# Output weights of two gated networks: the rest of the split written by ScalarE and an accumulating transfer, and 15 instead of 12 block tiles

## The chip, the cores and the metric

The kernel runs on one core of a Trainium2 chip. The metric is the device time of one execution in microseconds (us), the median over several executions. Engines are named as the profile names them: PE is TensorE (matrix products; PEld is its weight load), DVE is VectorE, ACT is ScalarE, POOL is GpSimd, SP is SyncE, which in this kernel issues almost all transfers.

## The reference

Two decoder layers run over 512 tokens of width 1024, in float32. Layer 0 mixes tokens with a state-space model, layer 1 with forgetting attention, and each is followed by a gated network ("ConvFFN"). The change touches only the two gated networks:

```python
def conv_ffn(h, w_up, conv_w, conv_b, w_down):
    up = h @ w_up                       # 1024 -> 2 x 2816
    a, b = jnp.split(up, 2, axis=-1)
    S = a.shape[1]
    ap = jnp.pad(a, ((0, 0), (CONV_W - 1, 0), (0, 0)))
    a_conv = conv_b
    for i in range(CONV_W):             # causal, width 3
        a_conv = a_conv + ap[:, i:i + S] * conv_w[i]
    return (jax.nn.silu(a_conv) * b) @ w_down      # 2816 -> 1024
```

Before each network a modulation (shift, scale and gate, three 1024 x 3072 products of a conditioning vector) and an RMS norm are applied; after it, the result times the gate is added to the residual.

## The kernel before, in words

**Products in two parts.** Every float32 product is made of three faster ones. A weight tile is split into a rounded part `hi` (type float32r) and a rest `lo = w - hi`; activations likewise. `mms` (L300) issues three matmuls for each 128-row slice: `hi` with the activation's `hi`, `hi` with its `lo`, and `lo` with its `hi`. `put_parts` (L285) does the split: ACT writes `hi` (L287, an Activate with Copy), then DVE writes `lo = src - hi` (L288, a Tensor Tensor). `split` (L272) takes the two buffers, has SP load the raw weights (`raw`, L187), and calls `put_parts`; `weights` (L290) does this for one output tile of 128 columns.

**Buffers.** Raw weights go through 3 buffers (`raw`), `hi` and `lo` through 5 each (`w_hi`, and `w_lo0` to `w_lo4` in turn). A tile's buffer is free again when PE has finished the tile that stood five places earlier in the order.

**The gated network** (`ffn`, L597). The 2816 hidden channels are 22 tiles of 128, numbered f = 0 to 21. For each f the two up products (a and b) are made in one of two ways:

- *Whole*: `product` (L308) with `self.weights` for 2 outputs of 8 slices. On PE 2 x 8 x 3 products, each in two halves of 256 tokens, which are 96 matmuls of 256 columns. On ACT two `hi` of 1024 elements, on DVE two `lo`.
- *Block* (`quarters`, L529): a Strassen-like scheme in which seven products of quarter blocks take the place of eight: 7 x 4 x 3 = 84 matmuls of 256 columns. Sums and differences of weight blocks are made by DVE (four `sums`, L537), four operands are split (`w_hi<-raw`, two `w_hi<-sums`, and one quarter `a22`), ACT copies four products out of PSUM (`nm_h`, L573) and DVE adds them (`nm_t`, L537). PE goes on accumulating into a product's PSUM bank after ACT has copied it.

`WHOLE_TILES` lists the whole tiles of each network. Before the change it is f = 0 to 4, 8, 11, 14, 17, 20 in the first network (12 block tiles) and 0 to 3 in the second (18 block tiles).

The hidden tiles are gathered in groups of 6, 5, 6 and 5 (`GROUPS`). While the up products of group q are made, the down products of group q - 1 are made between them: 8 output tiles (`down`, matmuls of 512 columns, 18 of them for a group of six and 15 for a group of five), one or two after each f. So 24 of a network's 32 down weight tiles come between up tiles, and the last group's 8 come at the end. DVE then also adds the result to the residual (L378). In the first network, DVE further computes two rows of a later modulation (`ada_units`, L256) after each f from 6 on.

**Order.** The tile framework decides the order of instructions on each engine when the program is built; instructions of later tiles stand between those of earlier ones. Each engine then runs its list in order, waiting on semaphores. GpSimd's list has nothing in the gated networks but small memsets that fix addresses.

Of the kernel before, what the change touches and what calls it, by code (L numbers as in the profile page):

```python
# [8 lines left out]
F32 = mybir.dt.float32  # L9
F32R = mybir.dt.float32r  # L10
I32 = mybir.dt.int32
AF = mybir.ActivationFunctionType
ALU = mybir.AluOpType
# [32 lines left out]
ROWS_FROM = 0  # L46
GROUPS = (6, 5, 6, 5)
TAIL = 4
WHOLE_TILES = (0, 1, 2, 3, 4, 8, 11, 14, 17, 20), (0, 1, 2, 3)
SUMS = (0,) * 6 + (2,) * 16  # L50
FIRST = (("c", (KT,)), ("s5_prm", (3, G // 2)))
REST = (
# [11 lines left out]
class Trunk:  # L64
# [6 lines left out]
    def __init__(self, tc, io, ctx):  # L71
        self.tc, self.nc, self.io, self.ctx = tc, tc.nc, io, ctx
        nc = self.nc
        pool = lambda name, bufs, **k: ctx.enter_context(tc.tile_pool(name=name, bufs=bufs, **k))
        self.const = pool("const", 1)
        self.act = pool("act", 1)
        self.wpool = pool("wpool", 3)
        self.tmp = pool("tmp", 2)
        self.small = pool("small", 2)
        self.dram = pool("dram", 1, space=DRAM)  # L80
        self.mm = pool("mm", 4, space=PSUM)
        self.aux = pool("aux", 4, space=PSUM)
        self.bg, self.late = [], ()
        self.acc = None
        self.pending = None
        self.rests, self.odd = 0, False

        self.ones = self.const.tile([P, P], F32, name="ones")
        nc.vector.memset(self.ones, 1.0)
        self.sc = self.const.tile([P, KT], F32, name="sc")  # L90
        self.ada = pool("ada", 1)
        self.crow = self.ada.tile([P, D], F32, name="ada_c")
        self.sc32 = self.const.tile([P, KT, 32], F32, name="sc32")

        self.sel = self.const.tile([P, 6], F32, name="sel")
        nc.gpsimd.memset(self.sel, 0.0)
        for q in range(4):
            for c in (q, 4 + q % 2):
                nc.gpsimd.memset(self.sel[32 * q:32 * q + 1, c:c + 1], 1.0)
        self.par = [self.const.tile([P, 24], F32, name=f"par{i}") for i in range(4)]  # L100
        self.ga = [self.const.tile([P, KT], F32, name=f"ga{i}") for i in range(4)]
# [170 lines left out]
    def split(self, src, shape, pool=None, bufs=WB, off=None):  # L272

        if off:
            more = TAIL_ROOM - math.prod(shape[1:])
            hi, lo = (self.wide(pool, n, {"bufs": bufs}, F32R, more, off[n], shape) for n in ("w_hi", "w_lo"))
        elif pool:
            hi, lo = (pool.tile(shape, F32R, name=n, bufs=bufs) for n in ("w_hi", "w_lo"))
        else:
            hi = self.wpool.tile(shape, F32R, name="w_hi", bufs=WB)  # L280
            lo = self.rest(shape, odd=self.odd)
        self.put_parts(hi, lo, self.raw(shape, src))
        return hi, lo

    def put_parts(self, hi, lo, src):  # L285
# [311 lines left out]
    def ffn(self, i, l, x, nxt, whole, sums=()):  # L597

        nc, tc = self.nc, self.tc
        with tc.tile_pool(name=f"ffn{l}", bufs=1, reuse_waits="tile") as pool:  # L600
            first = [sum(GROUPS[:q]) for q in range(len(GROUPS) + 1)]
            keep, g = {}, {}

            def gate_room(q):
                g[q] = [pool.tile([P, GROUPS[q], S], F32R, name=n, tag=f"{n}{q % 2}") for n in ("ghi", "glo")]

            self.gap(pool, 32, "g_gap")
            gate_room(0)
            b = [pool.tile([P, KT // 2, S], F32, name=f"x{j}", tag=n) for j, n in enumerate(("ghi1", "glo1"))]
            conv = pool.tile([P, 4, FT], F32, name="conv_wb")  # L610
            nc.sync.dma_start(conv, self.io["conv"][l])
            cw, cb = conv[:, :3], conv[:, 3]

            def gated(m, ps, cols):
                f = m // 2
                if m % 2 == 0:
                    t = pool.tile([P, S], F32, name="conv", bufs=2)
                    nc.scalar.activation(t, ps, AF.Identity, bias=cb[:, f:f + 1], scale=cw[:, 2, f:f + 1])
                    for d in (1, 2):
                        nc.vector.scalar_tensor_tensor(  # L620
                            t[:, d:], ps[:, :S - d], cw[:, 2 - d, f:f + 1], t[:, d:], op0=ALU.mult, op1=ALU.add
                        )
                    nc.scalar.activation(t, t, AF.Silu)
                    keep[f] = t
                    return
                t = keep.pop(f)
                nc.vector.tensor_tensor(t, t, ps, ALU.mult)
                q = sum(f >= n for n in first[1:])
                j = f - first[q]
                if q not in g:  # L630
                    gate_room(q)
                hi, lo = g[q]
                self.put_parts(hi[:, j, :], lo[:, j, :], t)

            after, y = nxt

            def up(fs, **k):
                self.odd = True
                self.product(
                    self.io["w_up"][l], range(2 * fs[0], 2 * fs[-1] + 2), KT, x, gated, apart=True, **k  # L640
                )
                self.odd = False

            last = len(GROUPS) - 1
            down = lambda q, ms, **k: self.product(
                self.io["w_down"][l][:, :, first[q]:first[q + 1], :], ms, GROUPS[q], g[q],
                self.add_residual(i, q == last), after=after, **k
            )
            todo, ready = [], {}
            for q, n in enumerate(GROUPS):  # L650
                for j, f in enumerate(range(first[q], first[q + 1])):
                    if f == 0:
                        up([0, 1], head=3)
                        todo.append(self.forms_x(pool, x, b))
                    elif f in whole:
                        if f > 1:
                            up([f], ready=ready)
                            ready = {}
                        if todo and f + 1 in whole:
                            self.odd = True  # L660
                            ready = {m: self.weights(self.io["w_up"][l][m], KT) for m in (2 * f + 2, 2 * f + 3)}
                            self.odd = False
                        for _ in range(3):
                            if todo and next(todo[0], True):
                                todo.pop()
                    else:
                        while todo:
                            if next(todo[0], True):
                                todo.pop()
                        self.quarters(pool, l, f, x, gated)  # L670
                    if q:
                        down(q - 1, range(j * KT // n, (j + 1) * KT // n))
                    self.tick(sums[f] if f < len(sums) else 0)
            self.done()
            down(last, range(KT), tail=TAIL, tail_pool=(pool, 4, TAIL_OFF))
        return y
# [827 lines left out]
def build(tc, io, out, stop=None):  # L1504
    with ExitStack() as ctx:
# [5 lines left out]
        k.bg = [k.ada_units(2, [0, 1]), k.ada_units(2, [2]), k.ada_units(3, [2])]  # L1511
        x = k.ffn(1, 0, x, k.norm_mod(2), WHOLE_TILES[0], SUMS)
        if stop == "ffn0":
# [3 lines left out]
        if stop == "fox":  # L1517
            return k.dump(out)
        k.ffn(3, 1, x, k.norm_out(out), WHOLE_TILES[1])
        k.finish_norm()  # L1520
# [82 lines left out]
```

## Time and profile before

| | |
|---|---|
| runs | 1197.50, 1193.79, 1190.88 us; median 1193.79 |
| the profiled execution | 1197.65 us; its span from first to last instruction 1195.9 us |
| granted TensorE clock, mean | 0.991 |
| PE busy | 1174.1 us (98%) |
| DVE busy | 988.7 us (83%) |
| ACT busy | 592.4 us (50%) |
| POOL busy | 62.6 us (5%) |
| DMA traffic | 183.83 MB, 154 GB/s mean |

The first network's up products begin at about 254 us and its last down product ends at about 602 us; the second's run from about 846 to 1186 us. A matmul's row in the profile is longer than the distance to the next row, because matmuls are pipelined: a 256-column matmul shows 276 ns but the next begins about 114 ns later. So PE's time is read from the distance between starts, or from windows, and not from the sum of its rows. In a table of windows each engine has its busy time in the window, with the number of its instructions in brackets, then the granted clock as a share, the DMA engines' busy share and what they moved. In a table of lines the number after the bar is the busy time in us, then the mean duration of one in ns, then the idle time ahead of them and what ended it.

### The profile page before, as it was taken

What the parts mean: (1) busy time and instruction counts of PE and PEld (TensorE: products, weight loads), DVE (VectorE), ACT (ScalarE), POOL (GpSimd) and SP (SyncE); (2) the same over time, 40 slices, a digit from 0 to 9 for tenths busy, and PEclk for the clock granted to TensorE, in tenths of its full rate; (3) what the DMA queues carried; (4) which work ended last, traced back from release to release, by engine and by line L of the source; (5) the groups of instructions that cost most, each with busy time, mean ns of one, the idle gap of its engine ahead of it and who ended that gap; (6) DMA issues with size and microseconds to landing.
All of it is one profiled execution on the core that took longest, in us unless ns stands there. A gap on an engine that the chain in (4) does not pass through costs nothing.

```text
span 1195.9 us, 21116 instructions
## 1 busy us (share of the span) xinstructions
PE 1174.1 (98%) x8243; PEld 1026.5 (86%) x8243; DVE 988.7 (83%) x1824; ACT 592.4 (50%) x1069; POOL 62.6 (5%) x114
## 2 busy tenths in 40 slices
PE   7999999999999999999999999999999999999997
PEld 2455687899999999999899788878999999999987
DVE  8899977889888888887776788866899888888855
ACT  2554525346544454453453566554466555555543
POOL 1000000000000000000000443330000000000000
PEclk9999989999999999999999999999999999999999
DMA  9687758822264455554514655523123342343331
GB/s 359 226 256 251 230 167 303 295 92 89 87 204 131 159 174 170 185 184 139 194 36 138 209 185 166 200 76 97 47 75 96 124 124 86 111 124 95 104 88 72
DMA packets 73234, 183.83 MB, mean 154 GB/s; under 512 B 23231, under 2 KB 25503, under 8 KB 72111
## 3 DMA queue, kind: packets, MB, share of 16 engines
q1 hardware_dynamic: 72847, 181.96, 46.6%
q8 instruction: 65, 1.06, 0.4%
q10 hardware_dynamic: 288, 0.52, 0.1%
q14 instruction: 34, 0.28, 0.1%
HBM read 175.53 MB, written 6.92 MB: 153 GB/s over the span
## 4 chain that ended last, share of the span: by engine, by line
PE 86%; DVE 7%; DMA 3%; ACT 2%; issue 1%; POOL 0%; SPq 0%; DVEq 0%; ACTq 0%; POOLq 0%
PE mmp L304 42%; PE mmp L566 15%; PE aux L566 6%; PE mmp L1167 4%; PE mmp L1344 3%; PE mmp L1197 2%; DVE w_lo L288 2%; PE aux L1490 2%; PE aux L1473 1%; PE aux L1061 1%; PE aux L1053 1%; PE mmp L221 1%; PE aux L1443 1%; ACT w_hi L287 1%; DMA raw<-in_w_down 1%
## 5 line engine op out<-in xcount | busy, mean ns | idle before, releaser
L287 ACT ACTIVATE w_hi<-raw 128x1024 fp32r<-128x1024 f32 (+4 forms) x197 | 176.0, 900 | 146.9 <-PE mmp L304 75.5
L288 DVE TENSOR_TENSOR w_lo<-raw,w_hi 128x1024 fp32r<-128x1024 f32 (+4 forms) x197 | 203.4, 1036 | 29.7 <-ACT w_hi L287 25.2
L304 PE MATMUL mmp<-a_hi,w_hi 128*128 128x256 f32 (+1 forms) x600 | 185.9, 311 | 0.0
L304 PE MATMUL mmp<-a_hi,w_lo 128*128 128x256 f32 (+1 forms) x600 | 182.8, 306 | 0.0
L304 PE MATMUL mmp<-a_lo,w_hi 128*128 128x256 f32 (+1 forms) x600 | 182.7, 305 | 0.0
L304 PE MATMUL mmp<-ghi,w_hi 128*128 128x512 f32 (+1 forms) x392 | 143.9, 367 | 0.0
L304 PE MATMUL mmp<-glo,w_hi 128*128 128x512 f32 (+1 forms) x392 | 143.9, 367 | 0.0
L304 PE MATMUL mmp<-ghi,w_lo 128*128 128x512 f32 (+1 forms) x392 | 143.6, 366 | 0.0
L304 PEld LDWEIGHTS mmp<-a_hi,w_hi 128*128 128x128 f32 x600 | 112.4, 188 | 7.6 <-issue 2.6
L304 PEld LDWEIGHTS mmp<-a_hi,w_lo 128*128 128x128 f32 x600 | 112.5, 188 | 6.4
L304 PEld LDWEIGHTS mmp<-a_lo,w_hi 128*128 128x128 f32 x600 | 112.6, 188 | 4.8
L287 ACT ACTIVATE w_hi<-sums 128x1024 fp32r<-128x1024 f32 x68 | 71.6, 1060 | 65.9 <-DVE sums L537 27.4
L566 PE MATMUL mmp<-w_hi 128*128 128x256 f32 x360 | 99.6, 277 | 0.0
L566 PE MATMUL mmp<-w_hi,w_lo 128*128 128x256 f32 x360 | 99.5, 276 | 0.0
L566 PE MATMUL mmp<-w_lo,w_hi 128*128 128x256 f32 x360 | 99.4, 276 | 0.0
L288 DVE TENSOR_TENSOR w_lo<-sums,w_hi 128x1024 fp32r<-128x1024 f32 x68 | 82.4, 1220 | 7.6 <-ACT w_hi L287 6.5
L256 DVE CUSTOM_DVE_ANT_0 ada_raw<-ada_raw,ada_c,rest 128x1024 f32<-128x1024 f32 x64 | 83.7, 1326 | 5.1 <-DMA ada_raw<-in_ada_rows 5.1
L304 PEld LDWEIGHTS mmp<-ghi,w_lo 128*128 128x128 f32 x392 | 73.6, 188 | 12.3
L304 PEld LDWEIGHTS mmp<-ghi,w_hi 128*128 128x128 f32 x392 | 73.6, 188 | 11.2
L304 PEld LDWEIGHTS mmp<-glo,w_hi 128*128 128x128 f32 x392 | 73.6, 188 | 11.1
L378 DVE SCALAR_TENSOR_TENSOR h<-mmp,par,h 128x512 f32<-128x512 f32 (+1 forms) x98 | 62.9, 649 | 23.4 <-PE mmp L304 23.3
L566 PEld LDWEIGHTS mmp<-w_hi 128*128 128x128 f32 x360 | 67.6, 188 | 0.1
(317 smaller groups left out, 2833.0 us busy)
## 6 DMA issues: line engine op xcount, KB each, us to landing
raw<-in_w_up SPq DMA_DIRECT2D x88, 512.0 KB, 3.4
ada_raw<-in_ada_rows SPq DMA_DIRECT2D x64, 512.0 KB, 4.2
raw<-in_ada_w SPq DMA_DIRECT2D x32, 512.0 KB, 5.5
raw<-in_w_down SPq DMA_DIRECT2D x32, 384.0 KB, 3.2
raw<-in_w_down SPq DMA_DIRECT2D x32, 320.0 KB, 3.1
nf<-nfd SPq DMA_DIRECT2D x8, 1152.0 KB, 5.7
raw<-in_fox_qk SPq DMA_DIRECT2D x16, 512.0 KB, 3.2
h<-in_x SPq DMA_DIRECT2D x8, 512.0 KB, 5.5
```

The source lines that it names most:

```text
L221: self.last_mm = nc.tensor.matmul(ps[32 * qq:32 * qq + 32, :], self.sc32[:, k, :], w[:, q * S:(q + 1) * S], start=(step is steps[0]), stop ...
L256: nc.vector.tensor_tensor_reduce(w, w, self.crow, 1.0, self.ada_b[:, i, m:m + 1], ALU.mult, ALU.add, self.par[i][:, m:m + 1])
L287: nc.scalar.activation(hi, src, AF.Copy)
L288: self.late = (nc.vector.tensor_tensor(lo, src, hi.bitcast(F32), ALU.subtract).ins,)
L304: self.last_mm = self.nc.tensor.matmul(o, wt, xt[:, cols], start=(k == 0 and n == 0), stop=(k == nk - 1 and n == 2),)
L378: self.nc.vector.scalar_tensor_tensor(h, v, self.par[i][:, 16 + m:17 + m], h, op0=ALU.mult, op1=ALU.add,).ins,
L566: self.last_mm = nc.tensor.matmul(o, wt[:, k], xt[:, k], start=(first and k == 0 and n == 0), stop=(k == H - 1 and n == 2), skip_group_che ...
L1053: nc.tensor.matmul(yp[g2][:, k, :], t[:, 2 * k + g2], u[:, g, :], start=(k == 0), stop=False, skip_group_check=True,)
L1167: nc.tensor.matmul(ps, w[m][:, k, :], x[:, k], start=(k == 0), stop=(k == KT - 1))
L1197: nc.tensor.matmul(gps[m], wt, xt[:, k], start=(k == 0 and part == 0 and xt is yhi), stop=(k == KT - 1 and part == 1))
L1344: self.last_mm = nc.tensor.matmul(ps[q, b][:, :n], xt[:, k, tb], wt, start=(k == 0 and i == 0), stop=(k == KT - 1 and i == 2),)
L1490: nc.tensor.matmul(pv[:, c * P:], self.v[:, hp, k, r].rearrange("p t d -> p (t d)"), pp[:, r, c + 3 * k:NB + 3 * k, :].rearrange("p b t -> ...
```

## The change

Two things are changed. For the 24 down tiles of each network that are made between up tiles (48 in all), `lo` is no longer made by DVE: ACT writes `-hi` into `lo`'s buffer with a second Activate, and then a transfer issued by GpSimd reads the weights from DRAM once more and adds them to what stands there, which gives `w - hi`. The last group's down tiles, and all up tiles, are split as before. And the first network's whole tiles are now 0 to 4, 10 and 16, so that tiles 8, 11, 14, 17 and 20 become block tiles and 10 and 16 whole ones: 15 block tiles for 12.

```diff
-WHOLE_TILES = (0, 1, 2, 3, 4, 8, 11, 14, 17, 20), (0, 1, 2, 3)
+WHOLE_TILES = (0, 1, 2, 3, 4, 10, 16), (0, 1, 2, 3)
...
-        self.rests, self.odd = 0, False
+        self.rests, self.odd, self.by_dma = 0, False, False
...
             hi = self.wpool.tile(shape, F32R, name="w_hi", bufs=WB)
             lo = self.rest(shape, odd=self.odd)
-        self.put_parts(hi, lo, self.raw(shape, src))
+        t = self.raw(shape, src)
+        if self.by_dma:
+            self.nc.scalar.activation(hi, t, AF.Copy)
+            self.nc.scalar.activation(lo, hi.bitcast(F32), AF.Copy, scale=-1.0)
+            self.nc.gpsimd.dma_start(lo, src, accum_op=ALU.add)
+        else:
+            self.put_parts(hi, lo, t)
         return hi, lo
...
                     if q:
+                        self.by_dma = True
                         down(q - 1, range(j * KT // n, (j + 1) * KT // n))
+                        self.by_dma = False
```

On PE the order of the work stays, but for the five tiles that become block tiles and the two that become whole ones. On ACT and POOL the lists move as follows. ACT, first network, at the tiles of the second group (`conv`, `ghi` and `nm_h` belong to the up tiles, `w_hi<-raw 128x640` are the down weights), before:

```order
L573 ACTIVATE nm_h<-aux 128x256
L287 ACTIVATE w_hi<-raw 128x512
L287 ACTIVATE w_hi<-raw 128x640
L623 ACTIVATE conv<-conv 128x512
L287 ACTIVATE ghi<-conv 128x512
L287 ACTIVATE w_hi<-raw 128x640
L573 ACTIVATE nm_h<-mmp 128x256 x2
```

and with the change (line numbers are higher by six behind the new lines; L284 is `hi`, L285 is `-hi`):

```order
L579 ACTIVATE nm_h<-aux 128x256
L293 ACTIVATE w_hi<-raw 128x512
L284 ACTIVATE w_hi<-raw 128x640
L285 ACTIVATE w_lo<-w_hi 128x640
L629 ACTIVATE conv<-conv 128x512
L284 ACTIVATE w_hi<-raw 128x640
L293 ACTIVATE ghi<-conv 128x512
L285 ACTIVATE w_lo<-w_hi 128x640
L579 ACTIVATE nm_h<-mmp 128x256 x2
```

Each down tile now has a second instruction on ACT, right behind `hi` or with one instruction of an up tile between them; the copies `nm_h` of the next block tile stand behind it.

POOL, the first network, before:

```order
L136 MEMSET x_gap 128x16
L136 MEMSET ehi_gap 128x16
L136 MEMSET v_gap 128x32
```

and with the change:

```order
L136 MEMSET x_gap 128x16
L136 MEMSET ehi_gap 128x16
L286 DMA w_lo<-in_w_down 128x768 x8
L286 DMA w_lo<-in_w_down 128x640 x8
L286 DMA w_lo<-in_w_down 128x768 x8
L136 MEMSET v_gap 128x32
```

The 24 transfers stand in POOL's list with nothing between them, in the order in which PE uses the tiles; in the second network they stand the same way, at the end of the list.

## The prediction

> **What bounds the kernel now.** I read the page's busy shares first, then the chain of waits over a piece of the first network, then windows over both networks.
>
> ```profile
> PE 1174.1 (98%) x8243; PEld 1026.5 (86%) x8243; DVE 988.7 (83%) x1824; ACT 592.4 (50%) x1069; POOL 62.6 (5%) x114
> ```
>
> ```profile
> 25 pieces in order of time: start us, us, what
> 459.81 2.75 PE mmp L566 x24
> 462.56 1.36 PE aux L566 x12
> 463.92 2.72 PE mmp L566 x24
> 466.64 1.36 PE aux L566 x12
> 468.00 1.36 PE mmp L566 x12
> 469.36 3.42 PE mmp L304 x15
> ```
>
> ```profile
> 310.30:564.00 253.70, 253.70 (x1863) 238.99 (x1862) 216.20 (x320) 119.38 (x178) 0.52 (x1) 1.00 0.51 165
> 891.00:1148.00 257.00, 256.71 (x1882) 241.67 (x1882) 221.93 (x329) 140.40 (x221) 0.00 (x0) 1.00 0.35 109
> ```
>
> The chain names nothing but PE in the gated networks: one product follows the other, at a granted clock of 1.00. In the window of the first network PE is busy for 253.70 of 253.70 us, in that of the second for 256.71 of 257.00. DVE is busy for 85% and 86% of them, ACT for 47% and 55%, the DMA engines for 0.51 and 0.35, POOL has nothing. So the time of both networks is the number of matmuls times their distance, and work taken from DVE is by itself worth nothing: what can be won is what PE is spared.
>
> **The change part by part.** *Three more block tiles.* A whole tile (96 matmuls), the down tile after it, a block tile (84 matmuls) and its down tile, in windows of the first network:
>
> ```profile
> 445.32:456.23 10.91, 10.91 (x97) 10.91 (x96) 8.93 (x14) 3.42 (x4) 0.00 (x0) 1.00 0.59 185
> 456.23:459.65 3.42, 3.42 (x18) 2.82 (x16) 2.54 (x5) 0.76 (x2) 0.00 (x0) 1.00 0.07 29
> 459.65:469.20 9.55, 9.55 (x86) 9.55 (x84) 9.09 (x13) 5.16 (x8) 0.00 (x0) 1.00 0.55 175
> 469.20:472.61 3.41, 3.41 (x17) 2.82 (x16) 2.95 (x6) 2.44 (x5) 0.00 (x0) 1.00 0.04 15
> ```
>
> 10.91 - 9.55 = 1.36 us a tile, 12 matmuls at 0.114 us. Three tiles: **4.1 us** less. It is the only term on the path.
>
> *DVE.* Its groups in the first network from the second group's up tiles on (329.4 to 564 us):
>
> ```profile
> L288 DVE TENSOR_TENSOR w_lo<-raw,w_hi 128x1024 fp32r<-128x1024 f32 x19 | 23.1, 1222 | 1.6 <-ACT w_hi L287 1.2
> L288 DVE TENSOR_TENSOR w_lo<-sums,w_hi 128x1024 fp32r<-128x1024 f32 x19 | 23.1, 1221 | 4.3 <-ACT w_hi L287 4.2
> L288 DVE TENSOR_TENSOR w_lo<-raw,w_hi 128x768 fp32r<-128x768 f32 x15 | 14.3, 954 | 0.6 <-ACT w_hi L287 0.5
> L537 DVE TENSOR_TENSOR sums<-raw 128x512 f32<-128x512 f32 x18 | 11.9, 688 | 4.1 <-DMA raw<-in_w_up 4.1
> L537 DVE TENSOR_TENSOR nm_t<-mmp,nm_h 128x256 f32<-128x256 f32 x30 | 11.8, 418 | 0.0
> L288 DVE TENSOR_TENSOR w_lo<-raw,w_hi 128x640 fp32r<-128x640 f32 x10 | 8.2, 821 | 0.7 <-ACT w_hi L287 0.7
> L288 DVE TENSOR_TENSOR w_lo<-raw,w_hi 128x512 fp32r<-128x512 f32 x10 | 6.9, 686 | 0.0
> ```
>
> Removed: 16 rests of 954 ns and 8 of 821 ns, 21.8 us a network. Added: a block tile has one rest from raw (1.22), two from sums (2.44), a quarter's (0.69), four sums (4 x 0.69) and four additions (4 x 0.42), 8.8 us, a whole tile two rests (2.44): 6.3 us more, 19.0 for three. The first network's DVE load falls by 2.8 us, the second's by 21.8. On the path both are 0, since PE covers them. Blocks now come five in a row (5 to 9, 11 to 15, 17 to 21) where they came in pairs, but each leaves DVE 1.2 us less to do, so a run should build up no more lag than a pair did. The 0.3 us for which PE is not busy in the second network may go; I leave it at 0.
>
> *ACT.* The window of ACT's work about a block tile and PE's need of it:
>
> ```profile
> 466.17 0.36 ACT L573 ACTIVATE nm_h<-mmp 128x256 f32<-128x256 f32 x1
> 473.60 0.72 ACT L287 ACTIVATE w_hi<-raw 128x640 fp32r<-128x640 f32 x1
> 474.23 0.37 ACT L573 ACTIVATE nm_h<-mmp 128x256 f32<-128x256 f32 x1
> 483.88 0.85 ACT L287 ACTIVATE w_hi<-raw 128x768 fp32r<-128x768 f32 x1 [1.60 <-DMA raw<-in_w_down]
> ```
>
> ```profile
> 467.84 0.28 PE L566 MATMUL mmp<-w_hi 128*128 128x256 f32 x1
> 486.03 0.39 PE L304 MATMUL mmp<-ghi,w_lo 128*128 128x512 f32 x1
> ```
>
> `-hi` has the shape of `hi`: 16 x 0.85 + 8 x 0.72 = 19.4 us more a network. A block tile's four operands and four copies are another 3.2 us more than a whole tile's two operands (the windows above: 5.16 against 3.42 in PE's time alone, the rest beside the down tiles), some 10 us for three. ACT goes from 119.4 to about 149 us in the first network, below 60%, and in the second from 140.4 to 160, 62%. That is no bound, but ACT runs in order: `-hi` stands in front of the copies `nm_h` of the next block tile, and PE waits for these before it goes on in their bank. The copy of 466.17 ends at 466.53 and PE needs it at 467.84: 1.3 us to spare. One `-hi` of 0.72 to 0.85 fits into that. Cost 0; if two come together, 0.4 us at such a tile.
>
> *The transfer.* Its `lo` must be there when PE reads it. The tile whose `hi` starts at 473.60 is the second down tile after the block tile of 472.61, and PE reads its `lo` first at 486.03, 11.7 us after `hi` ended; 11.0 are left behind its `-hi`. In general a buffer comes free five places earlier: behind a block tile that is one block and one down tile, 9.55 + 3.41 = 12.96 us for a group of five, 9.55 + 18 x 0.227 = 13.6 for a group of six (0.227 is 3.41 over its 15 matmuls). Less `hi` and `-hi`, **11.0 to 12.0 us** are left for POOL's issue, the transfer, and what ACT puts in between. Behind a whole tile it is 1.4 us more.
>
> No row shows an accumulating transfer, nor one that POOL issues. The nearest are the plain loads of the same tiles, and the longest landing in the kernel:
>
> ```profile
> raw<-in_w_down SPq DMA_DIRECT2D x32, 384.0 KB, 3.2
> raw<-in_w_down SPq DMA_DIRECT2D x32, 320.0 KB, 3.1
> s_c<-in_s_c SPq DMA_DIRECT2D x1, 512.0 KB, 10.8
> ```
>
> It cannot beat the plain load: 3.2 us at least. It must read what stands in the buffer as well, so I take twice that, **6.4 us**; 10.8, the longest landing of a load in this trace, is the upper end. Even 10.8 is within 11.0, if `-hi` follows `hi` at once and POOL issues at once. POOL has nothing else in its list there, so no other work waits behind its waits but the next transfer, which is needed later. Cost 0 at 6.4 us; with the cover gone, each microsecond that it is late costs PE a microsecond at every run of down tiles behind a block: 14 in the first network, 16 in the second.
>
> [...]
>
> *The transfers' bytes.* 16 x 0.39 + 8 x 0.33 = 8.9 MB more a network, 35 GB/s on 165 in the first. If each byte takes the engines twice the time, their share goes from 0.51 to about 0.73: the loads that SP issues land somewhat later, and raw weights have their own lead (in the row of 483.88 ACT waited 1.60 us for one, and PE lost nothing). Cost 0.
>
> **Sum**, against the profiled execution: 1197.65 - 4.1 = 1193.55 us. Its span of 1195.9 becomes 1191.8, with the same 1.75 us around it. The runs' median of 1193.79 is 0.3% below the profiled time, and in the same proportion the forecast is 1189.7 us, 0.34% less.
>
> **The rivals.** *The transfer is late, and the kernel slower.* The place is PE's first `lo` of a down tile behind a block. It decides from about 11.5 us between `-hi` and landing, and a delay of e costs 30 x e, since the buffers turn at PE's pace and a stall at one tile does not shorten the next turn. At 0.14 us late the gain is gone; at 0.34 us the kernel is 0.5% slower; at 1 us it is 1197.65 - 4.1 + 30 = 1223.6, 1219.7 as a median. For it: the price has no row, the upper end of 10.8 lies only just inside, and `conv` or `ghi` stands between `hi` and `-hi` in places and waits for DVE there. Against it: 6.4 leaves 4.6 us at the tightest tile.
>
> [...]
>
> *ACT's copies are late.* Two tiles' `-hi` before a copy: 0.4 us at perhaps half of the 30 block tiles is 6 us. The first blocks of the second network had no room at all:
>
> ```profile
> 929.84 0.38 PE L566 MATMUL mmp<-a_hi,w_hi 128*128 128x256 f32 x1 [0.29 <-ACT nm_h L573]
> ```
>
> That makes 1197.65 - 4.1 + 6 = 1199.6, 1195.7 as a median: no difference that can be told. For it: the order of ACT shows `-hi` directly ahead of two copies. Against it: 1.3 us of room at most tiles, and DVE, for which ACT often waits, has less to do.
>
> *More is won than PE is spared.* It would need stalls of PE that the windows don't show (0 and 0.3 us); only the spread of the runs, 6.6 us in three, makes a measured gain over 0.5% possible.
>
> **How the numbers follow.** About 0.5%, 6 us, is what a measurement can tell from no change. The forecast of 1189.7 has 0.66, the late transfer 0.22, the late copies 0.08, more won 0.04. The forecast lies 1.9 us short of the bound for faster, so I move 0.06 of its chance there: faster 0.10, same 0.68, slower 0.22. Range: below, 4 us under the forecast for the spread, 1185.5; above, a transfer at the upper end and half of the 30 places late by 1 us, 15 us on 1193.55, is 1208.6, or 1204.7 as a median: 1206. What is left out is about half of the late case and little below.
>
> **What would show it.** Right: windows over both networks with PE busy throughout, block tiles of 9.55 us, 36 matmuls fewer, the transfers landing within 11 us, ACT near 60%. Wrong: PE rows that wait for a landing of `w_lo<-in_w_down` (late transfer) or for `nm_h` (late copies). A gain or loss of over 0.5% would make the prediction wrong.

## The result, and the profile after

The changed kernel is slower: 1200.23 us against 1192.56 us (medians of 16 runs each), ratio 1.0061, 95% interval 1.0044 to 1.0077. The forecast was 1189.7 us and no difference that can be told. The direction was wrong. The time lies inside the range only by luck: its upper end had been set for transfers late at 15 places, and one transfer was late.

The two profiled executions, 1197.65 us before and 1196.59 us after, hide this: the state-space stage, which the change does not touch, took 254.4 us in the first and 247.6 us in the second (to the start of the first network's first product). Read by stages, the first network took 347.3 us before and 349.9 after, the attention between the networks 244.1 and 244.2, the second network 339.7 and 342.7. So both networks are longer, by 2.6 and 3.0 us, though the first has 36 matmuls less.

The busy shares of the changed kernel (page, part 1), and windows over about the same stretches of its two networks as in the prediction:

```profile
PE 1168.1 (98%) x8207; PEld 1019.8 (85%) x8207; DVE 966.3 (81%) x1806; ACT 634.4 (53%) x1135; POOL 104.1 (9%) x162
303.50:554.80 251.30, 250.11 (x1826) 235.00 (x1826) 212.43 (x325) 144.73 (x220) 21.32 (x26) 1.00 0.71 200
885.00:1146.00 261.00, 258.41 (x1892) 242.73 (x1891) 204.02 (x308) 157.80 (x246) 20.94 (x24) 1.00 0.55 141
```

DVE fell, ACT rose to 58% and 60%, the DMA engines' share in the first network went from 0.51 to 0.71: all much as worked out. But PE, whose gaps there were 0 and 0.3 us before, now idles for 1.2 and 2.6 us, and a third gap lies behind the first window. What PE waited for (waits of PE, whole program, those of the networks):

```profile
PE aux L401 <- DVE ssq L371: 2.6, 1, 2.6
PE mmp L310 <- DMA w_lo<-in_w_down: 2.1, 1, 2.1
PE mmp L572 <- ACT nm_h L579: 1.6, 3, 1.0
```

**The end of the first network.** The largest loss. PE's timeline there, after and before (the last product of the first half, then the sums of squares that it must wait for):

```profile
583.27 0.28 PE L310 MATMUL mmp<-ghi,w_lo 128*128 128x256 f32 x1
586.13 1.01 PE L401 MATMUL aux<-ones,ssq 128*128 128x1 f32 x4 [2.58 <-DVE ssq L371]
```

```profile
592.48 0.28 PE L304 MATMUL mmp<-ghi,w_lo 128*128 128x256 f32 x1
593.06 0.61 PE L395 MATMUL aux<-ones,ssq 128*128 128x1 f32 x4 [0.31 <-DVE ssq L365]
```

The stall grew from 0.31 to 2.58 us, and it brought a second loss with it. Windows of the changed kernel behind the stall (PEclk is the number in front of the DMA share):

```profile
577.00:586.00 9.00, 6.55 (x58) 6.35 (x56) 6.86 (x13) 4.08 (x7) 0.00 (x0) 0.98 0.54 178
586.00:588.00 2.00, 1.87 (x8) 1.88 (x9) 0.47 (x2) 0.42 (x1) 0.00 (x0) 0.50 0.00 0
590.00:592.00 2.00, 2.00 (x10) 2.00 (x11) 1.32 (x7) 0.00 (x0) 0.00 (x0) 0.50 0.01 4
594.00:597.48 3.48, 3.48 (x32) 3.48 (x32) 3.13 (x9) 2.07 (x5) 0.00 (x0) 1.00 0.03 7
```

From 585.73 us on, just before the stall ended, TensorE was granted half its clock for 6.83 us. From the last block tile to the next stage ("the last stretch" below) it is 42.7 us instead of 37.7: 5.0 us, of which 2.3 are the longer stall and 2.7 are left for the clock. The chain of waits, followed back from the stall, leads through a plain load, and later through one of the next stage's weights, after and before:

```profile
552.42 5.38 DMA raw<-in_w_down
557.83 0.75 ACT w_hi L293
571.05 5.51 DMA raw<-in_fox_v
```

```profile
561.63 3.75 DMA raw<-in_w_down
565.40 0.75 ACT w_hi L287
578.66 4.83 DMA raw<-in_fox_v
```

The loads of `in_w_down` were both issued 2.4 us ahead of this stretch; the one took 5.4 us, the other 3.75. Those 1.6 us and the 0.7 us of the later load make up the 2.3 us.

**The second network's first transfer.** PE's timeline at its first down tile:

```profile
915.86 0.40 PE L310 MATMUL mmp<-glo,w_hi 128*128 128x512 f32 x1
918.37 0.50 PE L310 MATMUL mmp<-ghi,w_lo 128*128 128x512 f32 x1 [2.11 <-DMA w_lo<-in_w_down]
```

**Block tiles of the first network.** One took 10.79 us and one 10.09 instead of 9.55. ACT's timeline at the first:

```profile
428.62 1.06 ACT L293 ACTIVATE w_hi<-sums 128x1024 fp32r<-128x1024 f32 x1 [2.67 <-DVE sums L543]
429.58 0.37 ACT L579 ACTIVATE nm_h<-mmp 128x256 f32<-128x256 f32 x1
```

The copy `nm_h` for which PE waits stands behind a rounding that waits for DVE's sum, and DVE's timeline has that sum's first step late for a load. While that load was under way (421.10 to 426.88 us), the DMA engines' share was 0.94:

```profile
426.89 0.69 DVE L543 TENSOR_TENSOR sums<-raw 128x512 f32<-128x512 f32 x1 [1.55 <-DMA raw<-in_w_up]
```

The loads as a whole (DMA issues of the page of the changed kernel, median landing last):

```profile
raw<-in_w_down SPq DMA_DIRECT2D x32, 384.0 KB, 4.0
w_lo<-in_w_down POOLq DMA_DIRECT2D x32, 384.0 KB, 6.5
raw<-in_w_down SPq DMA_DIRECT2D x32, 320.0 KB, 3.9
```

The plain ones were 3.2 and 3.1 us before. What DVE waited for the up weights shows it best: the group of its first sums, before and after (tables of lines, whole program):

```profile
L537 DVE TENSOR_TENSOR sums<-raw 128x512 f32<-128x512 f32 x60 | 39.3, 687 | 20.9 <-DMA raw<-in_w_up 20.8
L543 DVE TENSOR_TENSOR sums<-raw 128x512 f32<-128x512 f32 x66 | 43.6, 687 | 44.3 <-DMA raw<-in_w_up 44.3
```

One sum takes 687 ns on average in both (680 to 696 ns over the 60 before, 680 to 695 over the 66 after), so GpSimd's issuing did not slow this work of DVE; DVE waited twice as long for loads.

### The profile page after: what moved, and what is told of

It reads as the page before. It is cut to its first block, busy times and chain, and to the rows that moved or that the text cites. A ratio compares the mean times of both kernels' runs of the same rounds, so it can differ in the third digit from the quotient of the medians.

```text
span 1194.8 us, 21200 instructions
## 1 busy us (share of the span) xinstructions
PE 1168.1 (98%) x8207; PEld 1019.8 (85%) x8207; DVE 966.3 (81%) x1806; ACT 634.4 (53%) x1135; POOL 104.1 (9%) x162
## 3 DMA queue, kind: packets, MB, share of 16 engines
q0 software_dynamic: 6912, 17.83, 8.9%
## 4 chain that ended last, share of the span: by engine, by line
PE 76%; DVE 11%; DMA 6%; issue 3%; ACT 2%; POOL 0%; DVEq 0%; SPq 0%; ACTq 0%; POOLq 0%
PE mmp L310 38%; PE mmp L572 13%; PE aux L572 5%; PE mmp L1352 3%; PE mmp L1175 3%; DMA raw<-in_w_up 3%; DVE w_lo L294 3%; PE mmp L1205 2%; PE aux L1498 2%; PE aux L1481 1%; DVE sums L543 1%; PE aux L1069 1%; PE aux L1061 1%; DVE conv L626 1%; PE aux L1451 1%
## 5 line engine op out<-in xcount | busy, mean ns | idle before, releaser
L293 ACT ACTIVATE w_hi<-raw 128x1024 fp32r<-128x1024 f32 (+3 forms) x149 | 137.0, 922 | 110.0 <-PE mmp L310 45.6
L294 DVE TENSOR_TENSOR w_lo<-raw,w_hi 128x1024 fp32r<-128x1024 f32 (+3 forms) x149 | 158.2, 1064 | 29.3 <-ACT w_hi L293 25.1
L310 PE MATMUL mmp<-a_hi,w_hi 128*128 128x256 f32 (+1 forms) x504 | 159.4, 318 | 0.0
L310 PE MATMUL mmp<-a_hi,w_lo 128*128 128x256 f32 (+1 forms) x504 | 156.3, 311 | 0.0
L310 PE MATMUL mmp<-a_lo,w_hi 128*128 128x256 f32 (+1 forms) x504 | 156.1, 311 | 0.0
L286 POOL DMA_DIRECT2D w_lo<-in_w_down x48 | 42.0, 875 | 675.0 <-ACT w_lo L285 328.5
L310 PEld LDWEIGHTS mmp<-a_hi,w_hi 128*128 128x128 f32 x504 | 94.4, 188 | 7.5 <-issue 2.6
L310 PEld LDWEIGHTS mmp<-a_hi,w_lo 128*128 128x128 f32 x504 | 94.5, 188 | 6.4
L310 PEld LDWEIGHTS mmp<-a_lo,w_hi 128*128 128x128 f32 x504 | 94.6, 188 | 4.6
L543 DVE TENSOR_TENSOR sums<-raw 128x512 f32<-128x512 f32 x66 | 43.6, 687 | 44.3 <-DMA raw<-in_w_up 44.3
```

The source lines that it names most:

```text
L286: self.nc.gpsimd.dma_start(lo, src, accum_op=ALU.add)
L293: nc.scalar.activation(hi, src, AF.Copy)
L294: self.late = (nc.vector.tensor_tensor(lo, src, hi.bitcast(F32), ALU.subtract).ins,)
L310: self.last_mm = self.nc.tensor.matmul(o, wt, xt[:, cols], start=(k == 0 and n == 0), stop=(k == nk - 1 and n == 2),)
L543: sub = lambda o, u, v, op=ALU.subtract: nc.vector.tensor_tensor(o, u, v, op)
```

## The experiments

Theory A: the transfers hold the DMA engines, plain loads land late, and PE stalls where a load has no lead. Theory B: the loss comes of five block tiles in a row. Theory C: it comes of the negations in ACT's order. Each run was timed beside the kernel before on the same chip; ratios are to it. The lengths of the networks are read from the one profiled execution of each, from the first product's start to the next stage, in the second network to the start of the last product:

| run | blocks, rests | ratio, 95% interval | first network | second network |
|---|---|---|---|---|
| before | 12, DVE | 1 | 347.3 | 339.7 |
| changed | 15, transfers | 1.0061 (1.0044 to 1.0077) | 349.9 | 342.7 |
| e1 | 12, transfers | 1.0043 (1.0019 to 1.0066) | 349.5 | 342.2 |
| e2 | 15, DVE | 1.0006 (0.9987 to 1.0024) | 352.4 | 341.6 |
| e3 | 15, transfers in the first network | 1.0042 (1.0021 to 1.0064) | 348.7 | 340.8 |
| e4 | e3, but for the end of the first | 1.0018 (0.9998 to 1.0039) | 349.3 | 341.0 |
| e5 | 12, negation on ACT, addition on DVE | 0.9994 (0.9976 to 1.0012) | 349.0 | 340.4 |
| e6 | 12, DVE, and idle adding transfers | 1.0176 (1.0148 to 1.0204) | 355.5 | 355.7 |
| e7 | 12, DVE, and idle plain transfers | 1.0032 (1.0010 to 1.0054) | 348.1 | 343.5 |
| e8 | 15, DVE, background units early | 0.9974 (0.9953 to 0.9995) | 345.1 | 341.3 |
| e9 | 12, DVE, units early | 0.9996 (0.9979 to 1.0012) | 348.0 | 340.6 |
| e10 | changed, units early | 1.0031 (1.0006 to 1.0056) | 350.6 | 343.1 |
| e11 | e10, one tile on DVE | 1.0034 (1.0012 to 1.0055) | 350.0 | 342.8 |
| e12 | e3, units early | 1.0005 (0.9975 to 1.0034) | 346.6 | 340.3 |

**Each half of the change alone.**

```diff
 e1, on the changed kernel
-WHOLE_TILES = (0, 1, 2, 3, 4, 10, 16), (0, 1, 2, 3)
+WHOLE_TILES = (0, 1, 2, 3, 4, 8, 11, 14, 17, 20), (0, 1, 2, 3)
 e2, on the kernel before
-WHOLE_TILES = (0, 1, 2, 3, 4, 8, 11, 14, 17, 20), (0, 1, 2, 3)
+WHOLE_TILES = (0, 1, 2, 3, 4, 10, 16), (0, 1, 2, 3)
```

> The rests of the down tiles as in the changed kernel (negation on ScalarE, accumulating transfer), the block tiles as before (12). Theory A, the transfers do the harm (they hold the DMA engines longer, so that plain loads land late, and the first one of the second network has too little lead): the 4.1 us of the blocks are not won, and the losses seen in the changed kernel stay: 3.0 us in the second network, 5.0 in the last stretch of the first, and some of the 1.7 at its blocks. 1201 to 1202 us against 1192.6, ratio 1.007 to 1.008. Theory B, the loss in the first network comes of the blocks that stand five in a row: only the 3.0 us of the second network are left, 1195.6 us, ratio 1.0025.

> 15 block tiles, all rests on VectorE as before, no accumulating transfer. Theory A: no plain load is late, the 4.1 us are won unless VectorE falls behind: 216.2 + 19 = 235 of 249.6 us in the first network, 94%. 1188.5 to 1190 us, ratio 0.997 to 0.998. Theory B: the 6.7 us lost in the first network of the changed kernel are lost here too, 1192.6 - 4.1 + 6.7 = 1195.2 us, ratio 1.002.

Measured 1198.54 us (1.0043) and 1194.8 us (1.0006). Neither theory has it alone. The transfers cost 0.4% without any new block (A, though less than its 0.7%), and the blocks win nothing without any transfer, though they spare 4.1 us: B comes near the size of that loss. In e2's profile PE lost 2.06 us at the end of the first network and 2.35 at a block tile:

```profile
PE mmp L566 <- ACT nm_h L573: 2.3, 1, 2.3
PE aux L395 <- DVE ssq L365: 2.1, 1, 2.1
```

```profile
303.50:557.70 254.20, 251.80 (x1827) 236.32 (x1826) 230.66 (x350) 126.86 (x196) 0.52 (x1) 0.99 0.51 164
```

DVE is at 91% there (230.66 of 254.20), where the kernel before had 85%, and the chain into the stall of 2.35 us is DVE's own work, without a load. At the same tile the changed kernel lost 0.5 us. So with 15 blocks DVE did need relief; the transfers gave it at a price of about the same size.

**Which part of the rest's new way hurts.**

```diff
 e5, on e1: no transfer
-            self.nc.gpsimd.dma_start(lo, src, accum_op=ALU.add)
+            self.late = (self.nc.vector.tensor_tensor(lo, t, lo.bitcast(F32), ALU.add).ins,)
 e6, on e1: rests on VectorE, the transfer into a buffer that nobody reads
-            self.nc.scalar.activation(hi, t, AF.Copy)
-            self.nc.scalar.activation(lo, hi.bitcast(F32), AF.Copy, scale=-1.0)
-            self.nc.gpsimd.dma_start(lo, src, accum_op=ALU.add)
+            self.put_parts(hi, lo, t)
+            ...
+            self.nc.gpsimd.tensor_copy(d[:, 0, 0:1], hi[:, 0, 0:1].bitcast(F32))
+            self.nc.gpsimd.dma_start(d, src, accum_op=ALU.add)
 e7, on e6: a plain transfer
-            self.nc.gpsimd.dma_start(d, src, accum_op=ALU.add)
+            self.nc.gpsimd.dma_start(d, src)
```

> 12 block tiles as before, no transfer: ScalarE writes the negated rounded part into lo, and VectorE adds the raw weights to it, at the price of its old subtraction. So only ScalarE's 38.8 us are added. Theory A (the transfers' hold on the DMA engines does the harm): about as before, 1193 us, ratio 1.000 to 1.001. Theory C (the negations stand in ScalarE's order ahead of the block tiles' copies, and these come late): the loss of the run with the transfers and 12 blocks, less its late first transfer in the second network, 1198.5 - 1.4 = 1197 us, ratio 1.003 to 1.004.

> The kernel before (12 blocks, rests on VectorE, no negation), and beside it the same 48 accumulating transfers of the same weights into a buffer that nobody reads; a copy of one column on GpSimd ties each to its tile's rounded part. Only the DMA engines' load is added. Theory A: the loss of the run with transfers and 12 blocks, less its late first transfer, 1197 us, ratio 1.003 to 1.004, with plain loads as late as there (90% of the second network's down loads within 6 us, where it was 3.8). Theory C: as before, 1192.7 us, ratio 1.000.

> As the run before this one, but the 48 transfers are plain ones of the same bytes, from the same queue. Theory A, where it is the doubled engine time of an accumulating byte that hurts: half the loss, 1194.8 us, ratio 1.002, and the share of the queue in the profile is half. If the bytes hurt and not the accumulating: as the run before this one.

Measured 0.9994, 1.0176 and 1.0032. The negation costs nothing that can be measured: C falls. The transfers cost even where nobody waits for them, and the adding ones far more than plain ones of the same bytes. Their queue on the pages of e6 and e7 (packets, MB, share of 16 engines):

```profile
q0 software_dynamic: 6912, 17.83, 9.7%
```

```profile
q0 software_dynamic: 3840, 17.83, 4.7%
```

The same 17.83 MB held the engines about 2.1 times as long when they were added (9.7% of 1215.0 us against 4.7% of 1196.7), and the page's median landing of the 384 KB transfers is 5.9 us against 4.3. DVE waited 44.6 us for up weights ahead of its first sums in e6, 31.0 in e7, 49.2 in e1, and 20.8 to 28.6 us in the kernels without transfers (before, e2, e5, e8, e9). In e6 PE waited 12.1 us in twelve places for `nm_h`, in e7 2.4 us in three. The size of e6 was not foreseen (1.003 to 1.004), and it is not that of e1 with the same transfers: there DVE had been relieved of the rests, here it was not, so late loads met a busy DVE. That this is the reason is argued, not shown. In e6 and e7 `hi` is also held until GpSimd has copied a column, and GpSimd waits for the transfer before (43.3 us in e6's second network, 33.0 in e7's). But no row of the waits of PE, DVE or ACT in the networks names GpSimd, and the waits of ACT for which the profile names nothing are 8.5 us in e6 and 13.5 in e7, so this hold does not explain the difference.

**Where.**

```diff
-                        self.by_dma = True
+                        self.by_dma = l == 0                              (e3)
+                        self.by_dma = l == 0 and f < 20                   (e4)
```

> The changed kernel with the second network's rests on VectorE again. Theory A: the second network is as before, 3.0 us less than in the changed kernel: 1197.2 us, ratio to the kernel before 1.004. If the 3.0 us were the spread of one execution: 1200.2 us, ratio 1.006.

> As the run before this one, and the last four down tiles beside up tiles of the first network (those of its last two up tiles) with their rests on VectorE too. Theory A: no transfer overlaps the loads of the last stretch, its stall of 2.6 us and the lowered clock behind it go, 5.0 us: 1192.2 us, ratio 0.9997. Theory B: the stall stays, 1197 us, ratio 1.004.

Measured 1198.4 and 1195.48 us. Without its transfers the second network takes 340.8 us; over the kernels of the table, e6 and e7 left out, it takes 339.7 to 341.6 without them and 342.2 to 343.1 with them. So they cost 2 us there, not 3: the kernel before happened to have its shortest second network in the profile. In e4 the stall at the end falls to 1.04 us and the clock stays, but 1.0 are more than the 0.3 of the kernel before, and PE waited another 3.6 us at block tiles of the first network in that execution. Theory A's 1192.2 was not reached.

**The end of the first network by itself.** Over the executions, that stall goes with the landing of two plain loads, those issued 3.7 and 2.4 us ahead of the stretch (3.6 and 2.3 in the expectations; DMA issues, PE's timeline and windows of each):

| execution | landings, us | PE stall, us | half clock behind it, us | the stretch, us |
|---|---|---|---|---|
| before | 3.7, 3.7 | 0.31 | 0 | 37.7 |
| e5 | 3.2, 3.4 | 0.46 | 0 | 37.9 |
| e7 | 4.4, 3.9 | 1.04 | 0 | 38.5 |
| e4 | 4.7, 4.2 | 1.04 | 0 | 38.5 |
| e1 | 5.1, 4.5 | 1.64 | 0 | 39.1 |
| e2 | 5.4, 4.9 | 2.06 | 6.8 | 42.3 |
| e3 | 5.7, 5.2 | 2.42 | 3.4 | 41.1 |
| changed | 5.9, 5.4 | 2.58 | 6.8 | 42.7 |
| e6 | 6.9, 6.1 | 3.25 | 6.8 | 43.3 |

Two background loads of 512 KB (`ada_raw`) are issued 7.4 and 6.2 us ahead of the stretch in all of these. So in the next five kernels the background units of the last two up tiles were done at two whole tiles:

```diff
 e8 (on e2), e10, e11, e12 (on the changed kernel)
-SUMS = (0,) * 6 + (2,) * 16
+SUMS = (0,) * 6 + (2,) * 4 + (4,) + (2,) * 5 + (4,) + (2,) * 3 + (0,) * 2
 e9 (on the kernel before)
+SUMS = (0,) * 6 + (2,) * 8 + (4,) + (2,) * 2 + (4,) + (2,) * 2 + (0,) * 2
 e11 and e12 besides
-                        self.by_dma = True
+                        self.by_dma = l == 0 or (q, j) != (1, 0)          (e11)
+                        self.by_dma = l == 0                              (e12)
```

> 15 block tiles with all rests on VectorE, and the four background units of the last two up tiles of the first network done two each at the whole tiles 10 and 16, so that their loads of 512 KB are not in flight when the last stretch's weights are loaded. In the run with 15 blocks and rests on VectorE the last stretch lost 2.1 us to a stall and 3.4 to the lowered clock behind it. Theory D, the stall there is set by the landing of the loads issued 3.6 and 2.3 us ahead of it (4.9 us there, 3.7 in the kernel before, which lost 0.4): they land in under 4 us, and 4 to 5 us come back: 1190 us, ratio 0.997 to 0.998. Theory E, the stall comes of VectorE's backlog from five blocks in a row, whatever the loads do: 1194.8 us, ratio 1.001.

> The kernel before (12 blocks, rests on VectorE) with the four background units of the last two up tiles done two each at the whole tiles 14 and 17. If the 3 us won by the 15 blocks with early units are the blocks', nothing much is won here: the last stretch of the kernel before lost 0.4 us to its stall, so 1192.2 to 1193, ratio 1.000. If they are the units', 1190 us, ratio 0.997.

Measured 0.9974 and 0.9996. In e8 the load issued 3.7 us ahead landed in 3.0 us and the stall was gone (PE's timeline and windows of e8):

```profile
584.60 0.61 PE L395 MATMUL aux<-ones,ssq 128*128 128x1 f32 x4
```

```profile
556.00:586.00 30.00, 29.89 (x168) 25.99 (x167) 20.99 (x32) 14.00 (x21) 0.00 (x0) 1.00 0.53 159
586.00:594.20 8.20, 8.10 (x71) 7.90 (x70) 6.78 (x25) 2.76 (x7) 0.31 (x1) 1.00 0.01 2
```

With 12 blocks the same move wins nothing, since there was nearly no stall to take away: the gain of e8 is that of the blocks, 0.26% (3.1 us) of the 4.1 us. Theory D is the landing of the loads, theory E DVE's backlog. E is not ruled out by this run. Ahead of the stretch DVE was as busy as in e2 (232.70 of 252.10 us by the window from the first block on), but the move took two things out of the stretch at once. In e2 the units themselves ran on DVE from 568.76 to 571.26 us, in the chain that leads to the stall; in e8 they ran earlier. Those 2.5 us would be enough for the 2.06 us by themselves. The table above speaks for the loads: in all its kernels the two units run in that stretch, and the stall goes with the landing. Which of the two e8 owes its time to was not separated. e8 is faster than both kernels, at 1191.51 us beside 1193.65 for the kernel before on that chip.

> The changed kernel with the four background units moved to the whole tiles 10 and 16, as in the run with rests on VectorE. Theory D (landing of the last stretch's loads): the loads issued 3.6 and 2.3 us ahead land in 4 us or less instead of 5.4 to 5.9, the stall of 2.6 us falls under 1.1 and the clock stays: 4 to 5 us less than 1200.2, 1195.5, ratio 1.002 to 1.003. If the two transfers issued 10 and 7 us ahead are enough to keep the loads late: a stall over 2 us stays, 1199 us, ratio 1.005.

> As the run before this one, and the first down tile of the second network with its rest on VectorE. Theory A (that transfer has too little lead, 9.2 us from hi to PE's first lo less negation, issue and landing): no stall of PE at that tile, 1.4 to 2.4 us less than the run before, 1193.5 us, ratio 1.001. If the stall only moves to the next down tile (12.0 us of lead): no difference.

> The changed kernel with the four background units moved, and the second network's rests on VectorE. Theory A: second network as in the kernel before, 3 us less than the changed kernel with early units: 1192.5 us, ratio 1.000, still above the 15 blocks with rests on VectorE and early units (0.9974), since the first network's loads land late beside its transfers and cost about 1.8 us at its blocks. If the first network's transfers pay once its end is mended: under 0.9974.

Measured 1.0031, 1.0034 and 1.0005. In all three that load landed in 3.4 to 3.8 us, there was no stall (0.1 us), and the stretch took 37.5 us, where the kernel before had 37.7: as theory D expected, though here too the move took the units' own work out of the stretch. But in e10 only 2.6 us of the 5.0 came back by the medians (3.6 by the ratios), since stalls appeared elsewhere (waits of PE in its first and in its second network):

```profile
PE mmp L572 <- ACT nm_h L579: 4.2, 3, 2.8
```

```profile
PE mmp L310 <- DMA w_lo<-in_w_down: 2.3, 1, 2.3
```

The longest lies behind whole tile 16, where the units now are. DVE waited there for one of their loads, and what stands behind it on ACT went late with it (DVE's and ACT's timelines of e10):

```profile
495.37 1.28 DVE L256 CUSTOM_DVE_ANT_0 ada_raw<-ada_raw,ada_c,rest 128x1024 f32<-128x1024 f32 x1 [1.27 <-DMA ada_raw<-in_ada_rows]
```

```profile
501.35 0.63 ACT L293 ACTIVATE ghi<-conv 128x512 fp32r<-128x512 f32 x1 [0.90 <-DVE conv L633]
501.89 0.83 ACT L284 ACTIVATE w_hi<-raw 128x768 fp32r<-128x768 f32 x1
502.75 0.84 ACT L285 ACTIVATE w_lo<-w_hi 128x768 fp32r<-128x768 f32 x1
503.50 0.64 ACT L579 ACTIVATE nm_h<-mmp 128x256 f32<-128x256 f32 x2
```

Here the negation does stand in the way of the copies, but only because ACT came to it late. In e11 the stall at the second network's first tile is gone, and stalls of 0.35 to 0.59 us at four places of the next 16 us are there instead (two of them also in kernels without transfers there), so the time is the same: the second of its two expectations. e12 against e8 leaves the transfers of the first network alone in question: 1.0005 against 0.9974. Their intervals overlap; by the centres alone the transfers would cost 3.7 us more than DVE's subtractions once the end is mended. That is not shown.

## Why the prediction was wrong

**"Three tiles: 4.1 us less. It is the only term on the path."** Block tiles of 9.55 us and 36 matmuls fewer came as said. That nothing else was on the path is false. "A run should build up no more lag than a pair did" counted on a DVE that is relieved; without the relief, in e2, the whole 4.1 us were lost, and 2.35 us of it at the second block tile of the last run, so already at a pair. With the relief the changed kernel still lost 0.5 us at that tile, with DVE's own work as the chain.

**The transfers' bytes: "their share goes from 0.51 to about 0.73 ... Cost 0."** This is the step that failed. The share was right (0.71), and twice the engine time a byte, the author's estimate, was right (2.1 by e6 and e7). The mistake was to price a mean. The engines were busy in bursts (0.94 in the 5.8 us of the late load shown above), and beside the transfers the loads of `in_w_down`, whose median landing had been 3.2 us, took a median of 4.0, and 5.9 and 5.4 us at the end of the first network. Alone, with 12 blocks, the transfers cost 0.43%, 5.1 us (e1). "Raw weights have their own lead" is true at most tiles. It is not true at the end of the first network, whose loads go out 2.4 to 3.7 us ahead, nor at block tiles, where DVE's sum waits for the load and ACT's copies wait behind it. The row with which I covered the step (ACT waiting 1.60 us for a load, PE losing nothing) was one with room.

**The transfer's lead: "11.0 to 12.0 us are left".** The price, the author's estimate of twice the plain load's 3.2 us, was right: 6.4 us taken, medians of 6.5 and 5.9 us measured for 384 and 320 KB, and POOL issues some 0.4 us after `-hi`. The lead was worked out from the turn of the buffers, which doesn't bind the second network's first down tile: ACT's row of its `hi` waits for no buffer, and only ACT's order says when it comes. The trace of before showed it: in the second network's first down tile `hi` ended at 913.4 us, and PE read `lo` at

```profile
920.28 0.39 PE L304 MATMUL mmp<-ghi,w_lo 128*128 128x512 f32 x1
```

That is 6.9 us, not 11. After the change it was 9.2 us from the end of `hi` to PE's delayed start, of which the landing took 7.2. So the rival of the late transfer came true at one place, not at thirty, and not with its price of 30 e: the next tile's transfer had its lead again, and PE lost 2.1 us once.

**ACT's copies are late.** PE did wait for `nm_h`, 1.6 us in three places, but not for the reason given: two negations cost nothing by themselves (e5). The copies stood behind a rounding that waited for DVE's sums. At the first of the two late block tiles (1.2 us) DVE waited for a load; at the second (0.5 us) its own list was late.

**A microsecond of stall costs a microsecond.** This stood behind every price, and it is too little. Over all 14 profiled executions 16 stalls of PE in the networks were longer than 1.3 us. The six under 2.0 us (one each in e1, e4 and e12, three in e6) left the clock at 1.00. Of the ten from 2.06 to 3.25 us, nine were followed by a granted clock of 0.50, six times for 3.41 us and three times, all at the end of the first network, for 6.83 us. The one of 2.11 us in the changed kernel's second network was not. At 0.50, half of such a time, 1.7 or 3.4 us, is by estimate the most that is added; in the last stretch it added 1.3 us (e3) and 2.6 to 2.8 us (changed, e2, e6): the table's stretch less its stall, beside 37.5 us with 0.1 us of stall in e10.

Where the stalls of 2.06 and 2.11 us stand against the changes of the granted clock tells them apart. In the traces of both kernels these changes stand on a grid of 3.413 us: in the changed kernel those at 43.01, 585.73, 592.55 and 1189.88 us are 159, 2 and 175 steps apart, in the kernel before those at 41.58, 45.00, 143.98, 157.64 and 1191.87 us 1, 29, 4 and 303. In e2, e6 and e10 windows date the starts of two times at 0.50 each, and they are 24, 153 and 122 steps apart. Windows on the grid about the stall of 2.06 us in e2, and about that of 2.11 us in the changed kernel, which lies across a border, with 0.56 us in one step and 1.55 in the next:

```profile
585.22:588.63 3.41, 1.35 (x13) 1.15 (x12) 2.13 (x6) 1.00 (x3) 0.00 (x0) 1.00 0.42 144
588.63:592.04 3.41, 3.41 (x16) 3.41 (x17) 0.33 (x1) 0.42 (x1) 0.00 (x0) 0.50 0.00 0
```

```profile
916.82:920.24 3.42, 1.87 (x8) 1.57 (x9) 3.42 (x6) 3.39 (x6) 0.00 (x0) 1.00 0.45 119
920.24:923.65 3.41, 3.41 (x24) 3.06 (x23) 3.29 (x5) 2.80 (x4) 0.87 (x1) 1.00 0.72 172
```

All eight stalls that put 2.06 us or more into one step were followed by a granted clock of 0.50 from the next step on. Of the other eight, the six under 2.0 us and that of 2.11 us (at most 1.55 us in one step) were not. The exception is e3's stall of 2.42 us, of 1.11 and 1.31 us; eight matmuls of a single column, which take 0.8 us, stand in its second step too. Whether an amount in one step decides it, and which between 1.55 and 2.06 us, was not shown.

**Smaller slips of the working.** The relief of 21.8 us over the 16 up tiles with down tiles behind them is 1.4 us each and not 1.2, and 4 us under the forecast is 1185.7. Neither changes the forecast.

**What stays open.** Why the last loads of the first network land later with 15 blocks and no transfer (5.4 us in e2) than with 12 (3.7 and 3.2 us in the kernel before and in e5): the loads issued in the 8 us ahead are the same ones, and each kernel has one profiled execution. Whether the late loads or the background units' work on DVE is the better thing to take out of that stretch. And how much of the transfers' cost in the first network is systematic: which block tiles stall, and by how much, differs between executions. The first network is built alike in e10, e11 and e12 and took 350.6, 350.0 and 346.6 us, so a length from one profile is good to some 4 us, and only the ratios tell smaller differences.

In sum for the changed kernel, from its one profile: in the first network 4.1 us won by the blocks, 5.0 lost at its end and 1.8 at two of its block tiles, together 2.7 lost (2.6 by its length); in the second 3.0, of which 2.1 are the stall at the first transfer. These 5.6 us lie near the 7.3 us that the ratio gives. By the ratios of the two halves, the transfers alone cost 5.1 us (e1) and the blocks alone won nothing, 0.7 us the other way (e2), where 4.1 had been forecast for both together.

## What to carry to other kernels

An engine's work that is handed to the DMA engines isn't free because their mean share leaves room (0.51 before the change here, and the transfers alone cost 0.43%, e1): look for the load with the least lead, and price the stall it causes there. Where a lead is worked out from the turn of buffers, the first tile and the last stretch need their own rows (6.9 us in the trace of before where 11.0 had been taken). And a stall of the matmul engine of 2 us or more should be priced with the slow clock behind it: nine of the ten from 2.06 to 3.25 us had a granted clock of 0.50 behind them, for 3.41 or 6.83 us.

## What had not been expected of the hardware

The accumulating transfers from GpSimd's queue held the DMA engines about 2.1 times as long as plain ones of the same bytes (9.7% of 1215.0 us in e6, 4.7% of 1196.7 in e7) and were cut into more packets (6912 against 3840), yet landed only 1.4 times as late (medians of 5.9 and 4.3 us for 384 KB). Issuing one took GpSimd 873 ns on average in e6, a plain one 542 in e7. Over all runs with adding transfers the median landing of 384 KB was 5.6 us (e12) to 6.6 (e11), under the other loads of these networks.

A short stall of the matmul engine was followed by a granted clock of 0.50, for 3.41 us or twice that, in all eight cases where 2.06 us or more of it fell into one step of the grid of 3.413 us (one each in the changed kernel and e11, two each in e2, e6 and e10).
